# Rotary embedding over eight batch rows: from five homes and whole-row VectorE steps to six homes and quarter-row steps

## The chip, the core and the metric

The kernel runs on one core of a Trainium2 chip. The metric is the device time of one execution in microseconds (us); three timed runs of the kernel before gave 316.1, 316.19 and 316.19, median 316.19. The engines that matter here are VectorE (DVE), ScalarE (ACT), GpSimd (POOL), which also issues most of the transfers, SyncE (SP), which issues two, and the core's 16 DMA engines.

## The reference

`x` is float32 of shape (8, 2048, 16, 64): batch, position, head, head dimension. `cos` and `sin` are float32 of shape (2048, 32). Neighbouring elements of the head dimension form a pair that is rotated by the position's angle:

```python
x1, x2 = x_pairs[..., 0], x_pairs[..., 1]
out1 = x1 * cos - x2 * sin
out2 = x1 * sin + x2 * cos
out = np.stack([out1, out2], axis=-1)      # float32, shape of x
```

Input and output are 67.1 MB each, and 8.39 MB of each belong to one batch row.

## The kernel before, in words

Each of the 128 partitions holds K = 16 positions of a batch row, 1024 values each (16 heads of 64), so one row is 128 x 16384 values. In SBUF a row is kept as bf16 in a "home", a slice of the tile `xt`; there are NX = 5 homes, and `HOME` (L37) says which row lives where: rows 5, 6 and 7 take homes 0, 1 and 2 again. A load (L68 to L70, issued by POOL) casts float32 to bf16 in the transfer, a store (L72 to L74, POOL) casts back.

Row 0 is split at the start. Its first four positions come as float32 through SP's queue (L101) into a staging tile `head`, and ScalarE casts them (L108). Its other twelve (L102), `cos` (L103), `sin` (L104), rows 1 and 2 (L105) and rows 3 and 4 (L106) are queued by POOL one behind the other. VectorE makes two bf16 tables out of `cos` and `sin` (L110 to L112); `s_tab` has the sign folded in.

`rotate` (L76) then does a row in three VectorE instructions: `qt` = row times `s_tab` (L89), row times `c_tab` in place (L92), and row plus `qt` with the two of each pair swapped (L97). The tile `qt` is as large as a row. Row 0 is done as four positions and then twelve (L116, L117), all others as sixteen at once.

The order of the issues is written out by hand. The first store, of row 0 alone, is held back by two tiny ScalarE copies, called in the middle of row 2 (L119 to L122): the first reads the last element of row 2's `qt`, the second rewrites one element of home 0, which the store reads. A one-element POOL copy (`mark`, L126) reads the end of home 4, so that POOL waits for rows 3 and 4 to land. After it POOL issues the store of rows 1 and 2, the load of row 5 (L128, into row 0's home, so after row 0's store has landed) and of rows 6 and 7 (L129, after the store of rows 1 and 2 has landed), the store of rows 3 and 4 (L132) and of rows 5 and 6 (L136). POOL issues in this order and waits in it. Row 7 is cast by ScalarE to float32 in four pieces (L138) into `wide`, which lies over homes 3 and 4, and goes out through SP's queue in one store (L139).

Of the kernel before, what the change touches and what calls it, by code (L numbers as in the profile page):

```python
# [2 lines left out]

# [4 lines left out]


@with_exitstack  # L10
def kernel(
    ctx: ExitStack,
    tc: tile.TileContext,
    x: bass.AP,
    cos: bass.AP,
    sin: bass.AP,
    out: bass.AP,
):
    nc = tc.nc
    fp32 = mybir.dt.float32  # L20
    bf16 = mybir.dt.bfloat16
    mult = mybir.AluOpType.mult
    add = mybir.AluOpType.add

    B, S, H, D = x.shape
    P = 128
    K = S // P
    KP = 16
    D2 = D // 2
    HD = H * D  # L30
    NX = 5
    HEAD = 4
    PART = 4
    STAGE = 3


    HOME = [0, 1, 2, 3, 4, 0, 1, 2]  # L37

    x_t = x.rearrange("b (p k) h d -> b p k (h d)", p=P, k=K)
    out_t = out.rearrange("b (p k) h d -> b p k (h d)", p=P, k=K)  # L40
    x_r = x.rearrange("b (p k) h d -> p b (k h d)", p=P, k=K)
    out_r = out.rearrange("b (p k) h d -> p b (k h d)", p=P, k=K)
    cos_t = cos.rearrange("(p k) c -> p (k c)", p=P, k=K)
    sin_t = sin.rearrange("(p k) c -> p (k c)", p=P, k=K)

    consts = ctx.enter_context(tc.tile_pool(name="consts", bufs=1))
    stage = ctx.enter_context(tc.tile_pool(name="stage", bufs=1))

    xt = consts.tile([P, NX, K * HD], bf16)
    cos_sb = consts.tile([P, K * D2], fp32)  # L50
    sin_sb = consts.tile([P, K * D2], fp32)
    c_tab = consts.tile([P, K, D], bf16)
    s_tab = consts.tile([P, K, D], bf16)

    wide = (
        xt[:, STAGE : STAGE + 2]
        .rearrange("p a c -> p (a c)")
        .bitcast(fp32)
        .rearrange("p (k c) -> p k c", c=HD)
    )  # L60

    gate = consts.tile([1, 1], bf16)
    mark = consts.tile([1, 1], bf16)

    def home(b, k0=0, k1=K):
        return xt[:, HOME[b], k0 * HD : k1 * HD].rearrange("p (k c) -> p k c", c=HD)

    def load(b, n):  # L68
        h = HOME[b]
        nc.gpsimd.dma_start(out=xt[:, h : h + n], in_=x_r[:, b : b + n])  # L70

    def store(b, n):  # L72
        h = HOME[b]
        nc.gpsimd.dma_start(out=out_r[:, b : b + n], in_=xt[:, h : h + n])  # L74

    def rotate(b, k0=0, k1=K, between=None):  # L76
        nk = k1 - k0
        xp = home(b, k0, k1)
        qt = stage.tile([P, KP, HD], bf16, name="qt", tag="work")

        def rows(a):
            return a.rearrange("p k (h e) -> p k h e", h=H, e=D)

        def tab(a):
            return dataclasses.replace(
                a, offset=a.offset + k0 * D, ap=[a.ap[0], [D, nk], [0, H], [1, D]]
            )

        nc.vector.tensor_tensor(out=rows(qt[:, :nk]), in0=rows(xp), in1=tab(s_tab), op=mult)  # L89
        if between is not None:  # L90
            between(qt)
        nc.vector.tensor_tensor(out=rows(xp), in0=rows(xp), in1=tab(c_tab), op=mult)  # L92
        q_swap = dataclasses.replace(
            qt, offset=qt.offset + 1, ap=[qt.ap[0], [2, nk * HD // 2], [-1, 2]]
        )
        x3 = xp.rearrange("p k (a j) -> p (k a) j", j=2)
        nc.vector.tensor_tensor(out=x3, in0=x3, in1=q_swap, op=add)  # L97

    with tc.manual_schedule():
        head = stage.tile([P, HEAD, HD], fp32, name="st", tag="work")  # L100
        nc.sync.dma_start(out=head[:, :HEAD], in_=x_t[0, :, :HEAD])  # L101
        nc.gpsimd.dma_start(out=home(0, HEAD), in_=x_t[0, :, HEAD:])  # L102
        nc.gpsimd.dma_start(out=cos_sb, in_=cos_t)  # L103
        nc.gpsimd.dma_start(out=sin_sb, in_=sin_t)  # L104
        load(1, 2)  # L105
        load(3, 2)  # L106

        nc.scalar.copy(out=home(0, 0, HEAD), in_=head[:, :HEAD])  # L108
        s2 = s_tab.rearrange("p k (i j) -> p (k i) j", j=2)
        nc.vector.tensor_copy(out=s2[:, :, 0], in_=sin_sb)  # L110
        nc.vector.tensor_scalar_mul(s2[:, :, 1], sin_sb, -1.0)  # L111
        nc.vector.tensor_copy(  # L112
            out=c_tab.rearrange("p k (i j) -> p (k i) j", j=2),
            in_=cos_sb.to_broadcast([P, K * D2, 2]),
        )
        rotate(0, 0, HEAD)  # L116
        rotate(0, HEAD, K)  # L117

        def first_store(qt):  # L119
            nc.scalar.copy(out=gate, in_=qt[:1, KP - 1, HD - 1 :])  # L120
            nc.scalar.copy(out=xt[:1, HOME[0], :1], in_=xt[:1, HOME[0], :1])  # L121
            store(0, 1)  # L122

        rotate(1)
        rotate(2, between=first_store)
        nc.gpsimd.tensor_copy(out=mark, in_=xt[:1, 4, K * HD - 1 :])  # L126
        store(1, 2)
        load(5, 1)  # L128
        load(6, 2)  # L129
        rotate(3)  # L130
        rotate(4)
        store(3, 2)  # L132
        for b in range(5, B):
            rotate(b)
            if b == 6:
                store(5, 2)  # L136
        for k in range(0, K, PART):
            nc.scalar.copy(out=wide[:, k : k + PART], in_=home(B - 1, k, k + PART))  # L138
        nc.sync.dma_start(out=out_t[B - 1], in_=wide)  # L139


# [1 line left out]
_INS = ['x', 'cos', 'sin']  # L143
_OUTS = [((8, 2048, 16, 64), 'float32')]


# [23 lines left out]
```

## Time and profile before

| what | value |
|---|---|
| median of the timed runs | 316.19 us |
| the profiled execution's own time | 316.11 us |
| its span in the profile | 314.3 us |
| VectorE busy | 210.3 us (67%), 30 instructions |
| ScalarE busy | 19.3 us (6%), 8 instructions |
| POOL busy | 12.4 us (4%), 16 instructions |
| three VectorE instructions of a whole row | 8.69 us each |
| the same of four positions | 2.28 to 2.29 us each |

The profiled execution's own time is 1.8 us longer than its span, which starts with the first recorded instruction and ends with the last. The page gives, for each engine, busy time; then the span in 40 slices with the busy share of the DMA engines; the DMA queues; the chain of work that ended last; and groups of instructions with the idle time ahead of each and what ended it. Loads cast to bf16, and their bytes are counted at the smaller, bf16 side: a row is 4.19 MB as a load and 8.39 MB as a store, though as much of HBM is moved by each.

### The profile page before, as it was taken

The page shows a single profiled execution, that of the slowest core. Times are in us where ns is not written, and L with a number is a line of the kernel's source. Part 1 is how long each engine was busy: PE and PEld are TensorE (multiplying, and loading weights), DVE is VectorE, ACT ScalarE, POOL GpSimd, SP SyncE. Part 2 cuts the span into 40 slices and gives each one's busy share as a digit, 9 for nine tenths or more (in the row PEclk, how much of TensorE's full clock was granted, in tenths as well). Part 3 has the DMA queues.
Part 4 walks back from the last instruction along what each step waited for, and adds up shares of the span by engine and source line. Part 5 has one row for each costly group of instructions (what it writes and reads, how often), then busy time and mean ns, then how long its engine had stood idle before and what let it go on. Part 6 is the DMA issues. An engine that isn't in the chain of part 4 may idle for free.

```text
span 314.3 us, 114 instructions
## 1 busy us (share of the span) xinstructions
DVE 210.3 (67%) x30; ACT 19.3 (6%) x8; POOL 12.4 (4%) x16
## 2 busy tenths in 40 slices
DVE  0009995099999999999992299903999999200000
ACT  1030000000000000000000000000000000790000
POOL 4000000000002400000000000000000000000000
DMA  7999999999999999999999999999999999999996
GB/s 253 264 284 200 200 200 267 200 200 204 263 200 267 409 525 400 400 425 509 400 200 225 242 200 200 234 234 334 400 509 425 400 400 525 409 400 400 525 409 267
DMA packets 2512, 102.24 MB, mean 325 GB/s; under 512 B 208, under 2 KB 208, under 8 KB 336
## 3 DMA queue, kind: packets, MB, share of 16 engines
q0 software_dynamic: 2224, 91.75, 92.1%
q1 hardware_dynamic: 288, 10.49, 8.0%
HBM read 67.63 MB, written 67.11 MB: 429 GB/s over the span
## 4 chain that ended last, share of the span: by engine, by line
DVE 67%; another core or an unknown queue 11%; ACT 3%; ACTq 1%; issue 0%; DVEq 0%
DVE xt L92 22%; DVE xt L97 22%; DVE qt L89 22%; ACT xt L138 3%; ACTq L165 1%; DVE c_tab L112 0%; DVEq L89 0%; DVEq L92 0%
## 5 line engine op out<-in xcount | busy, mean ns | idle before, releaser
L89 DVE TENSOR_TENSOR qt<-xt,s_tab 128x16384 bf16<-128x16384 bf16 (+2 forms) x9 | 69.7, 7743 | 34.5 <-DMA xt<-in_x_dram 34.3
L92 DVE TENSOR_TENSOR xt<-xt,c_tab 128x16384 bf16<-128x16384 bf16 (+2 forms) x9 | 69.7, 7743 | 0.4
L97 DVE TENSOR_TENSOR xt<-xt,qt 128x16384 bf16<-128x16384 bf16 (+2 forms) x9 | 69.7, 7743 | 0.3
L138 ACT CAST xt<-xt 128x4096 f32<-128x4096 bf16 x4 | 14.1, 3601 | 171.7 <-DVE xt L97 171.7
L110 DVE CAST s_tab<-sin_sb 128x512 bf16<-128x512 f32 x1 | 0.5, 454 | 23.8 <-DMA sin_sb<-in_sin_dram 23.8
L74 POOL DMA_DIRECT2D out_dram<-xt x4 | 2.7, 670 | 184.9 <-ACT xt L121 93.4
L126 POOL COPY mark<-xt 1x1 bf16<-1x1 bf16 x1 | 5.0, 5019 | 2.6 <-DMA xt<-in_x_dram 2.6
L120 ACT COPY gate<-qt 1x1 bf16<-1x1 bf16 x1 | 0.2, 192 | 78.6 <-DVE qt L89 78.6
L70 POOL DMA_DIRECT2D xt<-in_x_dram x4 | 2.7, 696 | 43.1 <-DMA out_dram<-xt 43.1
L108 ACT CAST xt<-st 128x4096 bf16<-128x4096 f32 x1 | 3.6, 3605 | 13.1 <-DMA st<-in_x_dram 13.1
L108 ACT ACT_TABLE_LOAD x1 | 1.3, 1283 | 0.7 <-PEq L154 0.7
L102 POOL DMA_DIRECT2D xt<-in_x_dram x1 | 0.7, 680 | 0.8 <-PEq L165 0.8
L112 DVE CAST c_tab<-cos_sb 128x1024 bf16<-128x1024 f32 x1 | 0.7, 685 | 0.0
L103 POOL DMA_DIRECT2D cos_sb<-in_cos_dram x1 | 0.6, 569 | 0.0
L104 POOL DMA_DIRECT2D sin_sb<-in_sin_dram x1 | 0.6, 562 | 0.0
L111 DVE TENSOR_SCALAR s_tab<-sin_sb 128x512 bf16<-128x512 f32 x1 | 0.4, 444 | 0.0
L121 ACT COPY xt<-xt 1x1 bf16<-1x1 bf16 x1 | 0.2, 188 | 0.0
L154 POOL MEMSET const-float32-0.0<- 128x1 f32 x1 | 0.1, 99 | 0.2 <-issue 0.2
L154 POOL MEMSET const-bfloat16-1.0<- 128x1 bf16 x1 | 0.1, 102 | 0.0
L154 POOL MEMSET const-float32-1.0<- 128x1 f32 x1 | 0.1, 99 | 0.0
L154 POOL MEMSET const-uint8-127<- 128x1 uint8 x1 | 0.1, 99 | 0.0
## 6 DMA issues: line engine op xcount, KB each, us to landing
xt<-in_x_dram POOLq DMA_DIRECT2D x3, 8192.0 KB, 59.3
xt<-in_x_dram POOLq DMA_DIRECT2D x1, 4096.0 KB, 57.6
xt<-in_x_dram POOLq DMA_DIRECT2D x1, 3072.0 KB, 21.1
st<-in_x_dram SPq DMA_DIRECT2D x1, 2048.0 KB, 14.4
cos_sb<-in_cos_dram POOLq DMA_DIRECT2D x1, 256.0 KB, 21.2
sin_sb<-in_sin_dram POOLq DMA_DIRECT2D x1, 256.0 KB, 21.3
out_dram<-xt POOLq DMA_DIRECT2D x4, 49.9
out_dram<-xt SPq DMA_DIRECT2D x1, 30.0
```

What stands on the lines that cost most here:

```text
L70: nc.gpsimd.dma_start(out=xt[:, h : h + n], in_=x_r[:, b : b + n])
L74: nc.gpsimd.dma_start(out=out_r[:, b : b + n], in_=xt[:, h : h + n])
L89: nc.vector.tensor_tensor(out=rows(qt[:, :nk]), in0=rows(xp), in1=tab(s_tab), op=mult)
L92: nc.vector.tensor_tensor(out=rows(xp), in0=rows(xp), in1=tab(c_tab), op=mult)
L97: nc.vector.tensor_tensor(out=x3, in0=x3, in1=q_swap, op=add)
L102: nc.gpsimd.dma_start(out=home(0, HEAD), in_=x_t[0, :, HEAD:])
L103: nc.gpsimd.dma_start(out=cos_sb, in_=cos_t)
L108: nc.scalar.copy(out=home(0, 0, HEAD), in_=head[:, :HEAD])
L112: nc.vector.tensor_copy(out=c_tab.rearrange("p k (i j) -> p (k i) j", j=2), in_=cos_sb.to_broadcast([P, K * D2, 2]),)
L126: nc.gpsimd.tensor_copy(out=mark, in_=xt[:1, 4, K * HD - 1 :])
L138: nc.scalar.copy(out=wide[:, k : k + PART], in_=home(B - 1, k, k + PART))
L165: with _tile.TileContext(nc) as tc:
```

## The change

There are six homes in place of five. The staging tile, `cos` and `sin` have no tiles of their own any more; they lie in home 5 (`early`) until the load of row 5 overwrites them. `qt` holds four positions, and every row is done in four quarters, of three instructions each. The gate ahead of the first store now reads the end of row 2 after its last addition, and that store takes rows 0 and 1. The load of rows 3, 4 and 5 is one transfer. Stores are (0,1), (2,3), (4,5), then 6 through POOL and 7 through SP. Rows 6 and 7 are loaded one by one into homes 0 and 1. `mark` is gone. ScalarE casts row 7 quarter by quarter, each as soon as VectorE is through with it, into `wide`, which now lies over homes 2 and 3. In the core of the diff below, the lines that only rename are left out.

```diff
-    KP = 16
+    KP = 4
-    NX = 5
+    NX = 6
-    HOME = [0, 1, 2, 3, 4, 0, 1, 2]
+    HOME = [0, 1, 2, 3, 4, 5, 0, 1]
...
+    early = xt[:, NX - 1].bitcast(fp32)
+    head = early[:, : HEAD * HD].rearrange("p (k c) -> p k c", c=HD)
+    cos_sb = early[:, HEAD * HD : HEAD * HD + K * D2]
+    sin_sb = early[:, HEAD * HD + K * D2 : HEAD * HD + 2 * K * D2]
...
+    def rotate_row(b):
+        for k in range(0, K, KP):
+            rotate(b, k)
...
         load(1, 2)
-        load(3, 2)
...
-        rotate(0, 0, HEAD)
-        rotate(0, HEAD, K)
-
-        def first_store(qt):
-            nc.scalar.copy(out=gate, in_=qt[:1, KP - 1, HD - 1 :])
-            nc.scalar.copy(out=xt[:1, HOME[0], :1], in_=xt[:1, HOME[0], :1])
-            store(0, 1)
-
-        rotate(1)
-        rotate(2, between=first_store)
-        nc.gpsimd.tensor_copy(out=mark, in_=xt[:1, 4, K * HD - 1 :])
-        store(1, 2)
-        load(5, 1)
-        load(6, 2)
-        rotate(3)
-        rotate(4)
-        store(3, 2)
-        for b in range(5, B):
-            rotate(b)
-            if b == 6:
-                store(5, 2)
-        for k in range(0, K, PART):
-            nc.scalar.copy(out=wide[:, k : k + PART], in_=home(B - 1, k, k + PART))
-        nc.sync.dma_start(out=out_t[B - 1], in_=wide)
+        load(3, 3)
+        for b in range(3):
+            rotate_row(b)
+        nc.scalar.copy(out=gate, in_=home(2, K - 1, K)[:1, 0, HD - 1 :])
+        nc.scalar.copy(out=xt[:1, 0, :1], in_=xt[:1, 0, :1])
+        store(0, 2)
+        rotate_row(3)
+        store(2, 2)
+        load(6, 1)
+        load(7, 1)
+        rotate_row(4)
+        rotate_row(5)
+        store(4, 2)
+        rotate_row(6)
+        store(6, 1)
+        for k in range(0, K, KP):
+            rotate(7, k)
+            nc.scalar.copy(out=wide[:, k : k + KP], in_=home(7, k, k + KP))
+        nc.sync.dma_start(out=out_t[7], in_=wide)
```

More of the change, by code (lines that the diff above doesn't have):

```diff
@@ L27 @@
     K = S // P
-    KP = 16
+    KP = 4
     D2 = D // 2
     HD = H * D
-    NX = 5
+    NX = 6
     HEAD = 4
-    PART = 4
-    STAGE = 3
-    HOME = [0, 1, 2, 3, 4, 0, 1, 2]
+    HOME = [0, 1, 2, 3, 4, 5, 0, 1]
     x_t = x.rearrange("b (p k) h d -> b p k (h d)", p=P, k=K)
@@ L49 @@
     xt = consts.tile([P, NX, K * HD], bf16)
-    cos_sb = consts.tile([P, K * D2], fp32)
-    sin_sb = consts.tile([P, K * D2], fp32)
     c_tab = consts.tile([P, K, D], bf16)
     s_tab = consts.tile([P, K, D], bf16)
+    gate = consts.tile([1, 1], bf16)
+    early = xt[:, NX - 1].bitcast(fp32)
+    head = early[:, : HEAD * HD].rearrange("p (k c) -> p k c", c=HD)
+    cos_sb = early[:, HEAD * HD : HEAD * HD + K * D2]
+    sin_sb = early[:, HEAD * HD + K * D2 : HEAD * HD + 2 * K * D2]
     wide = (
-        xt[:, STAGE : STAGE + 2]
+        xt[:, 2:4]
         .rearrange("p a c -> p (a c)")
@@ L60 @@
     )
-    gate = consts.tile([1, 1], bf16)
-    mark = consts.tile([1, 1], bf16)
     def home(b, k0=0, k1=K):
@@ L74, in store, with rotate @@
         nc.gpsimd.dma_start(out=out_r[:, b : b + n], in_=xt[:, h : h + n])
[L76 to L79, printed above, removed]
+    def rotate(b, k0):
+        xp = home(b, k0, k0 + KP)
+        qt = stage.tile([P, KP, HD], bf16, name="qt", tag="qt")
         def rows(a):
@@ L85, in tab @@
             return dataclasses.replace(
-                a, offset=a.offset + k0 * D, ap=[a.ap[0], [D, nk], [0, H], [1, D]]
+                a, offset=a.offset + k0 * D, ap=[a.ap[0], [D, KP], [0, H], [1, D]]
             )
-        nc.vector.tensor_tensor(out=rows(qt[:, :nk]), in0=rows(xp), in1=tab(s_tab), op=mult)
-        if between is not None:
-            between(qt)
+        nc.vector.tensor_tensor(out=rows(qt), in0=rows(xp), in1=tab(s_tab), op=mult)
         nc.vector.tensor_tensor(out=rows(xp), in0=rows(xp), in1=tab(c_tab), op=mult)
         q_swap = dataclasses.replace(
-            qt, offset=qt.offset + 1, ap=[qt.ap[0], [2, nk * HD // 2], [-1, 2]]
+            qt, offset=qt.offset + 1, ap=[qt.ap[0], [2, KP * HD // 2], [-1, 2]]
         )
@@ L97, in rotate @@
         nc.vector.tensor_tensor(out=x3, in0=x3, in1=q_swap, op=add)
+    def rotate_row(b):
+        for k in range(0, K, KP):
+            rotate(b, k)
     with tc.manual_schedule():
-        head = stage.tile([P, HEAD, HD], fp32, name="st", tag="work")
-        nc.sync.dma_start(out=head[:, :HEAD], in_=x_t[0, :, :HEAD])
+        nc.sync.dma_start(out=head, in_=x_t[0, :, :HEAD])
         nc.gpsimd.dma_start(out=home(0, HEAD), in_=x_t[0, :, HEAD:])
@@ L105 @@
         load(1, 2)
-        load(3, 2)
-        nc.scalar.copy(out=home(0, 0, HEAD), in_=head[:, :HEAD])
+        nc.scalar.copy(out=home(0, 0, HEAD), in_=head)
         s2 = s_tab.rearrange("p k (i j) -> p (k i) j", j=2)
```

## The prediction, made before the changed kernel ran

> **What bounds the kernel now.** I read the page first: its slices and its DMA queues.
>
> ```profile
> DMA  7999999999999999999999999999999999999996
> q0 software_dynamic: 2224, 91.75, 92.1%
> q1 hardware_dynamic: 288, 10.49, 8.0%
> HBM read 67.63 MB, written 67.11 MB: 429 GB/s over the span
> DVE 67%; another core or an unknown queue 11%; ACT 3%; ACTq 1%; issue 0%; DVEq 0%
> ```
>
> The two queues' packets took 92.1% and 8.0% of the 16 DMA engines' span: together all of it. No slice but the first and the last is under 9. So the DMA engines never rest, and the span is the sum of the transfers. The last line is the chain of waits; it names VectorE, with 67%, but a chain follows who released whom, and VectorE waits three times for a load. I take the queue sums over the chain: a step of VectorE costs nothing so long as the DMA queue has the next transfer in hand when the one before ends. The whole question is whether it has, at each handover.
>
> Next the timeline, for the rate at which transfers end.
>
> ```profile
> 62.42 8.69 DVE L89 TENSOR_TENSOR qt<-xt,s_tab 128x16384 bf16<-128x16384 bf16 x1 [10.66 <-DMA xt<-in_x_dram]
> ...
> 97.32 0.19 ACT L120 COPY gate<-qt 1x1 bf16<-1x1 bf16 x1 [78.56 <-DVE qt L89]
> 97.33 8.69 DVE L92 TENSOR_TENSOR xt<-xt,c_tab 128x16384 bf16<-128x16384 bf16 x1
> 97.42 0.19 ACT L121 COPY xt<-xt 1x1 bf16<-1x1 bf16 x1
> 97.91 0.55 POOL L74 DMA_DIRECT2D out_dram<-xt  x1 [93.43 <-ACT xt L121]
> 101.04 5.02 POOL L126 COPY mark<-xt 1x1 bf16<-1x1 bf16 x1 [2.58 <-DMA xt<-in_x_dram]
> ...
> 120.67 0.57 POOL L70 DMA_DIRECT2D xt<-in_x_dram  x1 [4.92 <-DMA out_dram<-xt]
> ...
> 159.44 0.70 POOL L70 DMA_DIRECT2D xt<-in_x_dram  x1 [38.20 <-DMA out_dram<-xt]
> ```
>
> Rows 1 and 2 have landed at 62.42, rows 3 and 4 at 101.04: 38.62 for two, 19.31 a row. Row 0's store has landed at 120.67, that of rows 1 and 2 at 159.44: 38.77 for two, 19.4 a row. Sixteen row transfers of 19.3 to 19.4 are 309 to 310 us; with `cos`, `sin`, 1.7 us ahead of the first packet and about 1.2 behind the last that is the span.
>
> Last the windows of a quarter of a microsecond around the first handover from loads to stores. The two last columns are DMA share and GB/s; a packet is booked where it starts, so shares stand in bursts.
>
> ```profile
> 97.75:98.00 0.25, 0.25 (x1) 0.00 (x0) 0.09 (x1) 1.00 1.22 262
> 98.00:98.25 0.25, 0.25 (x1) 0.00 (x0) 0.25 (x1) 1.00 8.55 1835
> 98.25:98.50 0.25, 0.25 (x1) 0.00 (x0) 0.21 (x1) 1.00 0.00 0
> ...
> 100.25:100.50 0.25, 0.25 (x1) 0.00 (x0) 0.00 (x0) 1.00 3.69 1573
> 100.50:100.75 0.25, 0.25 (x1) 0.00 (x0) 0.00 (x0) 1.00 6.12 2622
> ```
>
> GB/s divided by the share tells loads from stores: 1835/8.55 is 215 (a load, counted in bf16), 2622/6.12 is 428 (a store). The last load packets start from 97.75 to 98.25, the first stores from 100.25 to 100.75, 2.45 later; a burst comes each 2.4 us while nothing is missing (19.3 us for eight of them), so there is no hole. The store that was issued at 97.91 was ready when the first engine came free, near 100.3.
>
> **The change, part by part.** All terms are set against the profiled execution's own 316.11 (span 314.3 and 1.8 around it), 0.08 under the median of 316.19.
>
> *Quarter steps on VectorE.* The four-position instructions of row 0 start at 25.05, 27.37, 29.69, and the next at 32.02: 2.32 each with the gap, against 8.73 for a whole row's (62.42 to 71.15). Four times 2.32 is 9.29, so a row is 27.87 in place of 26.18, 1.7 more. VectorE has 104 idle us in the span, and its work is covered by transfers, except where a store waits for it, below.
>
> *Loading three rows in one transfer, later.* The load of rows 3 to 5 overwrites `cos`, `sin` and the head, so POOL waits until the table casts end, at 25.1. Nothing is queued on POOL behind it but stores that come later still. The queue meanwhile works on rows 1 and 2, until 62: 37 us of cover, no cost. It ends one row later than the old load, at 101.04 + 19.31 = 120.35 by the landing, and its engines come free 0.3 to 0.8 before that (100.25 to 100.75 against 101.04): from 119.6 to 120.1, mean 119.8. Row 3 can't be used before the whole transfer lands, as its three rows share one wait: VectorE idles 118.2 to 120.4.
>
> *The first store, where the sum is decided.* Rows 1 and 2 now end at 62.42 + 24 x 2.32 = 118.1. The gate, which was released by row 2's first instruction, waits for its last. From there the old timeline holds: gate start 97.32 to issue 97.91 is 0.59, so POOL issues the store of rows 0 and 1 at 118.75. In the kernel before, the store was issued 2.4 before an engine came free; now 0.85 before the first and 1.05 before the mean. How long a POOL store takes from issue to its first packet when engines wait for it, the trace does not show. Bounds: it can't be over 2.45 for one row (97.91 to the first free engine, no hole); with a pair's issue of 0.70 in place of 0.55, 2.6. From below: SP's head load is issued at 0.74 and its first packets start in the slice 1.50 to 1.75, 1.0 after; its issue takes 0.37, so 0.63 remain behind it. POOL's 0.70 and 0.63 make 1.33; if packets start while the issue still runs, under 1.05, and then there is no hole. POOL's first load speaks for the longer side: issued at 1.25, its packets (215 GB/s a share) show only from 5.25 on, though behind some of the head's. I take the middle of 1.33 and 2.6, 1.97: the engines wait 1.97 - 1.05 = 0.9. A restart costs more than the wait: at the start of the span the first two bursts of packets lie about 1.1 apart, later ones 0.6, so the first packet is up to 0.5 longer; I take 0.2. Sum of this part: **+1.1 us**, from 0 to 2.0 (2.6 - 1.05 + 0.5). The queue is full from here to the end, so it goes into the time whole.
>
> [...]
>
> *The handovers behind it.* Row 3 is done at 120.5 + 12 x 2.32 = 148.4, and the store of rows 2 and 3 is issued at 148.7; the transfer ahead ends at 120 + 38.6 = 158.6: ten us of cover. If that cover is gone, lateness enters one for one. The load of row 6 waits for the first store to land, near 160, as the old load did; rows 2 and 3 go out until 197, so it is hidden, and so is row 7's, issued right behind. Rows 4 and 5 are done at 204.1; POOL's store of them is due at 236: 32 of cover. Row 6 lands at 217 and is done at 245, its store due at 275: 30. Row 7 is done at 273; ScalarE has only the last quarter's cast left (3.60), and SP issues at 277, while row 6's store runs until 294 even alone: 17. The two queues share the engines at the end, as before, where SP's store was issued at 283.46 and the share stood at 0.97 to 0.98 up to 310. The tail is the same.
>
> *What goes away:* the `mark` copy (5.02 on POOL) had 9 idle us behind it, worth nothing. No byte and no transfer is saved: 13 issues before, 13 after.
>
> Sum: 316.11 + 1.1 = **317.2 us**.
>
> **The rivals.**
>
> *No hole.* POOL's store is ready within about 1.05 us of its issue, or close enough that the hole stays under 0.7. For it: SP's 1.0; against: POOL's issue alone takes 0.70, and POOL's first load shows so late. It decides below a latency of 1.7. Time 316.1 to 316.8, not slower. Chance 0.34.
>
> *VectorE becomes late at the second store too.* If the quarter steps ran slower beside stores than the 2.32 that row 0 shows beside loads, row 3's twelve would use up the 10 us from 3.15 us a step on; at 3.3 the store would come 1.9 late, giving 319.1. Against: the whole-row steps took 8.69 beside loads (62.42) and beside stores (97.33) alike. Chance 0.04.
>
> *Faster.* If packets of a three-row load came closer than those of two-row ones, or the tail's two queues together moved more than 429 GB/s, a per cent of a row's 19.3 would be saved per row so moved; three rows would give 0.6, hence 315.5. Against: the DMA engines are at 100.1% by their own packets. Chance 0.03.
>
> **How the numbers follow.** The forecast, a hole at the first store and a time between 316.8 and 318.2, has 0.59. A measurement of this kernel tells about 0.2% from no change, 0.63 us: 315.6 to 316.8 counts as the same. Faster 0.03 (the last rival), same 0.34 (the no-hole rival), slower 0.63 (the forecast and late VectorE). The range runs from no hole, 316.1, to the bound of 2.0 us, 318.1, with 0.1 for the run's own spread: 316.1 to 318.2.
>
> **What would show it.** In the profile after: VectorE steps of 2.29 throughout, 221 us busy in all; POOL's first store issued near 118.75 with row 3 starting near 120.4; in fine windows around 120, a last burst of load packets near 117.4 and the first store burst 3.3 to 3.5 later rather than 2.4 (with no hole: near 119.8); every later burst 2.4 apart; DMA share sum a little under 100%; the span longer by just this hole. I am wrong if the store is issued before 118, if a hole shows elsewhere (148 to 160, or the tail), or if the packets themselves take another time than before.

## The result, and the profile after

The changed kernel takes 317.01 us (median of 9 runs, 316.94 to 317.23) against 316.19 us before: 0.82 us more, a ratio of 1.0026 with a 95% interval of 1.0017 to 1.0035. It is a little slower. The prediction said 317.2 within 316.1 to 318.2.

The profiled execution of the changed kernel took 317.23 us, the longest of the nine, with a span of 315.5; the spans of the others are 315.2 to 315.5. Its tables landed 0.25 us later than in the profile of before (VectorE's first cast starts at 24.02 against 23.77). This is the last of the 16 DMA engines and not all of them: by the packet starts in the trace, the engines' first full-size load packets (32,768 bytes) start at 23.20 on the mean, against 23.19 before, but the last of them at 23.63 against 23.32. The seven profiles of this kernel's variants below have the first cast at 23.76 to 23.91, those of the kernel before and its variants at 23.72 to 23.91. So the wider spread belongs to this one execution; it makes about 0.25 of the 1.2 us between the two spans.

The page's lines on the DMA engines, for the changed kernel:

```profile
DMA  8999999999999999999999999999999999999996
...
q0 software_dynamic: 2224, 91.75, 91.7%
q1 hardware_dynamic: 288, 10.49, 7.9%
q14 instruction: 1, 0.01, 0.0%
```

The same packets now fill 99.6% of the span in place of 100.1%. So some time is lost in which an engine has nothing to do. And there is a queue that the page of before does not have: q14, of the kind `instruction`, one packet; by the trace it has 8192 bytes and takes 0.34 us from 130.07 on. It is read here as code for one of the engines (an instruction fetch); the runs with added VectorE instructions, below, bear that out.

The timeline around the first store:

```profile
116.17 2.29 DVE L91 TENSOR_TENSOR xt<-xt,qt 128x4096 bf16<-128x4096 bf16 x1
118.49 0.19 ACT L115 COPY gate<-xt 1x1 bf16<-1x1 bf16 x1 [99.42 <-DVE xt L91]
118.59 0.19 ACT L116 COPY xt<-xt 1x1 bf16<-1x1 bf16 x1
119.08 0.73 POOL L71 DMA_DIRECT2D out_dram<-xt  x1 [92.39 <-ACT xt L116]
120.60 2.29 DVE L85 TENSOR_TENSOR qt<-xt,s_tab 128x4096 bf16<-128x4096 bf16 x1 [2.14 <-DMA xt<-in_x_dram]
```

POOL issues the store at 119.08, 0.33 later than forecast (118.75): VectorE waited for that last DMA engine and began row 1 at 62.67, not 62.42. The DMA engines' mean is not later. They come free at 119.78 (mean start of the last load packets, 117.35, and 2.43 that they took), as forecast (119.8). So the lead over the mean engine is 0.70 and not the forecast's 1.05. Windows of a quarter of a microsecond at the same place (engines' busy time, then the TensorE clock, DMA share and GB/s; a packet is booked where it starts):

```profile
117.00:117.25 0.25, 0.25 (x1) 0.00 (x0) 0.00 (x0) 1.00 3.04 655
117.25:117.50 0.25, 0.25 (x1) 0.00 (x0) 0.00 (x0) 1.00 4.87 1049
117.50:117.75 0.25, 0.25 (x1) 0.00 (x0) 0.00 (x0) 1.00 1.22 262
...
120.25:120.50 0.25, 0.00 (x0) 0.00 (x0) 0.00 (x0) 1.00 8.51 3670
120.50:120.75 0.25, 0.15 (x1) 0.00 (x0) 0.00 (x0) 1.00 1.22 524
```

The bursts give the number of packets: 655 GB/s for 0.25 us is 164 KB, five load packets of 32,768 bytes; 3670 is 14 store packets of 65,536. In the kernel before, the first stores started 2.45 us after the last loads. Here it is 3.08 on the mean of the 16 engines (packet starts in the trace). This is a hole of 0.63, at the place that was forecast. It also lines the engines up: the last loads started over 0.72 us, the first stores within 0.15. The engine that came free first lost about 0.9, the last one at most 0.3, and the last one sets the end.

The second loss was not forecast. The same view ten microseconds later:

```profile
130.00:130.25 0.25, 0.25 (x1) 0.00 (x0) 0.00 (x0) 1.00 9.27 3965
130.25:130.50 0.25, 0.25 (x1) 0.00 (x0) 0.00 (x0) 1.00 0.69 262
...
132.25:132.50 0.25, 0.25 (x1) 0.00 (x0) 0.00 (x0) 1.00 6.12 2621
132.50:132.75 0.25, 0.25 (x1) 0.00 (x0) 0.00 (x0) 1.00 3.06 1311
...
133.00:133.25 0.25, 0.25 (x1) 0.00 (x0) 0.00 (x0) 1.00 0.61 262
```

3965 GB/s for 0.25 us is 991 KB: 15 store packets (983 KB) and 8 KB more, the packet of q14. One of the 16 engines carries it, and this engine's store packet comes a window later, in the next burst two windows after the others. It never catches up, as every engine has the same work: by the trace the packets of 32,768 and 65,536 bytes come in 120 bursts of 16, one for each engine, up to the last. At the end of the span:

```profile
311.00:311.25 0.25, 0.00 (x0) 0.00 (x0) 0.00 (x0) 1.00 8.46 3670
311.25:311.50 0.25, 0.00 (x0) 0.00 (x0) 0.00 (x0) 1.00 0.60 262
...
311.75:312.00 0.25, 0.00 (x0) 0.00 (x0) 0.00 (x0) 1.00 0.60 262
```

Fifteen last packets start by 311.5, the sixteenth 0.6 after them, and the kernel waits for it. In the kernel before all sixteen lie within 0.34:

```profile
310.25:310.50 0.25, 0.00 (x0) 0.00 (x0) 0.00 (x0) 1.00 3.63 1573
310.50:310.75 0.25, 0.00 (x0) 0.00 (x0) 0.00 (x0) 1.00 6.04 2621
```

The other handovers went as forecast: the store of rows 2 and 3 was issued at 148.77 (148.7), row 6's at 246.26 (245), SP's at 277.53 (277), and none of them shows a hole.

### The profile page after: what moved, and what is told of

It reads as the page before. It is cut to its first block, busy times and chain, and to the rows that moved or that the text cites. A ratio compares the mean times of both kernels' runs of the same rounds, so it can differ in the third digit from the quotient of the medians.

```text
span 315.5 us, 185 instructions
## 1 busy us (share of the span) xinstructions
DVE 221.3 (70%) x99; ACT 19.6 (6%) x8; POOL 7.3 (2%) x15
## 4 chain that ended last, share of the span: by engine, by line
DVE 70%; another core or an unknown queue 8%; DMA 7%; ACT 1%; issue 1%; POOL 0%; DVEq 0%; PEldq 0%
DVE qt L85 23%; DVE xt L86 23%; DVE xt L91 23%; DMA xt<-in_sin_dram 7%; ACT xt L129 1%; POOL xt L99 0%; POOL xt L100 0%; DVE s_tab L106 0%; DVE s_tab L107 0%; DVEq L85 0%; DVE c_tab L108 0%; PEldq L156 0%
## 5 line engine op out<-in xcount | busy, mean ns | idle before, releaser
L85 DVE TENSOR_TENSOR qt<-xt,s_tab 128x4096 bf16<-128x4096 bf16 x32 | 73.3, 2292 | 26.4 <-DMA xt<-in_x_dram 25.4
L91 DVE TENSOR_TENSOR xt<-xt,qt 128x4096 bf16<-128x4096 bf16 x32 | 73.3, 2292 | 1.1
L86 DVE TENSOR_TENSOR xt<-xt,c_tab 128x4096 bf16<-128x4096 bf16 x32 | 73.3, 2292 | 1.1
L104 ACT CAST xt<-xt 128x4096 bf16<-128x4096 f32 x1 | 3.6, 3604 | 13.5 <-DMA xt<-in_x_dram 13.5
L108 DVE CAST c_tab<-xt 128x1024 bf16<-128x1024 f32 x1 | 0.7, 684 | 0.0
```

The lines of the kernel that those rows point to most:

```text
L85: nc.vector.tensor_tensor(out=rows(qt), in0=rows(xp), in1=tab(s_tab), op=mult)
L104: nc.scalar.copy(out=home(0, 0, HEAD), in_=head)
L108: nc.vector.tensor_copy(out=c_tab.rearrange("p k (i j) -> p (k i) j", j=2), in_=cos_sb.to_broadcast([P, K * D2, 2]),)
```

## The experiments

Theory A, formed on this profile, has two causes: the hole at the first store, and one instruction fetch that sets a single DMA engine back. Theory B: the hole is all of it. Theory C: neither, but the quarter steps or the start. The times of before that ran with these kernels have medians of 316.18 to 316.34.

**The changed kernel without a gate.**

```diff
-        nc.scalar.copy(out=gate, in_=home(2, K - 1, K)[:1, 0, HD - 1 :])
-        nc.scalar.copy(out=xt[:1, 0, :1], in_=xt[:1, 0, :1])
```

> The changed kernel without the two tiny ScalarE copies ahead of the first store, so that POOL issues it when row 1 is done, near 90.5, and not near 119. Theory A (two causes: the hole at the first store, 0.55 on the last DMA engine, and one 8192-byte instruction fetch near 130 that sets a single DMA engine back by 0.6): no hole near 120, the fetch still there with one engine ending 0.6 behind the other fifteen, time 316.4 to 316.7. Theory B (the hole is all of it, the fetch is absorbed): 316.1 to 316.3. Theory C (neither; quarter steps or another start cost it): 317.0.

It took 317.70 us, ratio 1.0044 (1.0032 to 1.0057): slower than with the gate, which no theory had. The store was issued at 90.69, and there is no hole; the windows show something else:

```profile
117.50:117.75 0.25, 0.25 (x1) 0.00 (x0) 0.00 (x0) 1.00 9.12 1442
117.75:118.00 0.25, 0.25 (x1) 0.00 (x0) 0.00 (x0) 1.00 4.17 655
...
120.75:121.00 0.25, 0.00 (x0) 0.00 (x0) 0.00 (x0) 1.00 4.30 1835
121.00:121.25 0.25, 0.00 (x0) 0.00 (x0) 0.00 (x0) 1.00 4.89 2097
```

1442 GB/s are 11 load packets, and their share of 9.12 is 0.83 for each, against 0.61 elsewhere. A share of one over 16 engines and 0.25 us is 4 us of packet time, so these last packets took 3.3 us each and not 2.43. This became theory D, which later kernels test: a store that is in the queue before the last load packets ahead of it start stretches them by 0.9. The fetch is there too, at 130.68.

**The kernel before in quarter steps.**

```diff
-        rotate(1)
-        rotate(2, between=first_store)
+        for k in range(0, K, 4):
+            rotate(1, k, k + 4)
+        for k in range(0, K, 4):
+            rotate(2, k, k + 4, between=first_store if k == 4 else None)
...
-            nc.scalar.copy(out=gate, in_=qt[:1, KP - 1, HD - 1 :])
+            nc.scalar.copy(out=gate, in_=qt[:1, 3, HD - 1 :])
```

Rows 3 to 7 are done in quarters in the same way.

> The kernel before with every row from 1 on in quarter steps, the first store gated on row 2's second quarter, so issued near 100.5 with an engine coming free near 100.3 or just after 99.8 if the gate is passed at its first multiplication; homes, loads and stores as before. Theory A: the fetch appears for VectorE's longer instruction stream and one DMA engine ends about 0.6 late, time 316.6 to 316.8, plus 0 to 1.5 if the first store's issue at 100 comes too late as well (a hole at 100.5 would show in the windows). Theory B: only such a hole counts, 316.2 without one. Theory C: 317.0 without a hole.

317.44 us, ratio 1.0037 (1.0025 to 1.0050). The store was issued at 100.17, and the engines came free from 100.70 on: first stores 2.93 after the last loads on the mean, a hole of 0.49. One fetch, at 173.75, sets one engine back by 0.5; it ends 0.45 behind the last of the others. In this profile the loads ahead of the hole had also lost 0.34 (the last load packets start at 98.42 on the mean, against 98.08 before; several between 81 and 94 us took 2.55 to 2.60 in place of 2.43). Why is open. It is a part of what this kernel takes more than the changed one. Both causes appear in the old order of rows and homes, so neither hangs on six homes or on the three-row load.

**The gate 9 us later.**

```diff
-        nc.scalar.copy(out=gate, in_=home(2, K - 1, K)[:1, 0, HD - 1 :])
+        rotate(3, 0)
+        nc.scalar.copy(out=gate, in_=home(3, KP - 1, KP)[:1, 0, HD - 1 :])
```

> The changed kernel with the gate ahead of the first store reading the end of row 3's first quarter in place of the end of row 2: VectorE reaches it near 127.6, so the store is issued near 128.1, 9.0 later. Theories A and B: the hole near 120 grows by 9.0 and nothing behind takes it up, so 326.0 (325.5 to 326.5). Theory C: the lateness is absorbed by later slack, 317 to 318.

325.60 us, ratio 1.0298 (1.0284 to 1.0312), 8.6 above the changed kernel. Theory C is out: what the first store is late by goes into the time. The store was issued at 128.08, 9.0 later; that 8.6 and not 9.0 came out is put down to the second cause, by these windows:

```profile
124.25:124.50 0.25, 0.25 (x1) 0.00 (x0) 0.00 (x0) 1.00 0.08 33
...
129.25:129.50 0.25, 0.25 (x1) 0.00 (x0) 0.00 (x0) 1.00 9.12 3932
129.50:129.75 0.25, 0.25 (x1) 0.00 (x0) 0.00 (x0) 1.00 0.61 262
```

33 GB/s are the 8 KB of the fetch alone: it falls into the hole, where it delays nobody, and the engines start the stores together and end within 0.15.

**Tiny VectorE instructions in the kernel before**: 69 one-element copies ahead of row 5, where VectorE waits 11.17 us for a load. With them it has 99 instructions, as in the changed kernel.

```diff
         store(3, 2)
+        for _ in range(69):
+            nc.vector.tensor_copy(out=mark2, in_=gate)
```

> [...] Theory A: one instruction fetch of 8192 bytes in the span, one DMA engine 0.6 behind, time 316.6 to 316.8. Theory B and C: 316.2, the copies being hidden in the idle time.

316.43 us against 316.18, ratio 1.0006 (0.9997 to 1.0015): by itself not clear of nothing, and under theory A's 316.6 to 316.8. The copies took 12.3 us in all, 0.18 each, and so outlast the wait: row 5 starts 1.2 later than before; no handover shows a hole. The profile has the fetch, at 175.45. The engine that it set back by 0.5 was one of the first of the 16, so it ends only 0.2 behind the one that was last before.

> The kernel before with 198 one-element VectorE copies, 60 ahead of row 1 and 69 ahead of rows 5 and 6 each, all within VectorE's waits for loads (0.14 each). Theory A: two or three instruction fetches of 8192 bytes, each of which sets one DMA engine back by 0.5; 316.5 if they fall on different engines, up to 317.5 if on one. Theory B (the fetch is absorbed): 316.2 to 316.3.

With 198 such instructions (60 ahead of row 1, 69 each ahead of rows 5 and 6; they read `c_tab` and not `gate`, and are busy for 0.14 each): 316.93 us, ratio 1.0025 (1.0016 to 1.0034). Two fetches, at 61.7 and 214.3, and both on one engine, which ends alone:

```profile
310.25:310.50 0.25, 0.00 (x0) 0.00 (x0) 0.00 (x0) 1.00 5.44 2359
310.50:310.75 0.25, 0.00 (x0) 0.00 (x0) 0.00 (x0) 1.00 2.42 1049
...
311.25:311.50 0.25, 0.00 (x0) 0.00 (x0) 0.00 (x0) 1.00 0.60 262
```

The first set it back by 0.51, the second by 0.54; it ends 0.78 behind the next. Homes, transfers and their order are those of before. VectorE's rows start later, row 1 by 0.7 (it waits for the engine that was set back), rows 5 and 6 by 1.7 and 1.4 (the copies outlast the wait), but no store comes too late for the DMA engines by it: the first, issued at 98.60 and so 1.6 ahead of the first free engine, follows its loads by 2.44, and no two bursts lie more than 2.46 apart on the mean, as before. So the fetches cost 0.75, less than theory A's 317.5 for two on one engine, and theory B is out.

**The lead of the first store.** Three kernels move the gate ahead, to row 2's last multiplication by `c_tab`, its last by `s_tab`, and the one by `s_tab` a quarter earlier:

```diff
         nc.vector.tensor_tensor(out=rows(xp), in0=rows(xp), in1=tab(c_tab), op=mult)
+        if between is not None:
+            between(xp[:1, KP - 1, HD - 1 :])
...
+        for k in range(0, K, KP):
+            rotate(2, k, first_store if k == K - KP else None)
```

> The changed kernel with the gate one VectorE instruction earlier, on row 2's last multiplication by the cosine table: the first store is issued near 116.75, 3.0 before an engine comes free (119.75), where the kernel before had 2.4. Theory A (hole and fetch): no hole, the last load packets still 2.43 long, the fetch near 130 remains with one engine about 0.5 late: 316.4 to 316.8. Theory D, from the run without a gate (a store that is in the queue before the last load packets start stretches them by 0.9): no stretch yet or a small one, as they start at 117.1, so about the same 316.6. Rival E (any early store costs 0.9 in this kernel, whatever its lead): 317.5.

> The same with the gate on row 2's last multiplication by the sine table: the store is issued near 114.4, 5.3 ahead. Theory A: 316.4 to 316.8. Theory D: the store's work is queued before the last load packets start, so these take 3.3 in place of 2.43, and 317.3 to 317.7. Rival E: 317.5.

> The same with the gate one quarter of row 2 earlier: the store is issued near 107.4, 12.3 ahead. Theory A: 316.4 to 316.8. Theories D and E: last load packets of 3.3, 317.3 to 317.7, as without a gate.

They took 316.81 (ratio 1.0018, 1.0009 to 1.0026), 317.74 (1.0041, 1.0029 to 1.0054) and 317.59 (1.0038, 1.0024 to 1.0051). The last two are too slow for the fetch alone (theory A's 316.4 to 316.8) and near theory D's 317.3 to 317.7. The first lies between, and so do its last load packets (2.45 to 3.2 us). A fourth kernel has no gate, and a tiny store early:

```diff
+        nc.sync.dma_start(out=out_t[7, :, K - 1, :D], in_=head[:, 0, :D])
         load(3, 3)
```

> The kernel without a gate, and in addition a tiny store (64 floats a partition, 32 KB, overwritten later by row 7's store) from SP near 15 us, so that the output has been written to once before the first large store. Theory F (the 0.9 in the last load packets is a first-store cost, of the first write to the output): gone, 316.4 to 316.8. Theory D (it comes from a store being queued long ahead, whatever went before): still there, 317.4 to 317.9.

317.54 us, ratio 1.0039 (1.0026 to 1.0052), the last loads as long as without it: theory F falls. The last kernel adds a delay to the first of these four, so that the lead (how long before the first DMA engine comes free the store is issued) comes near the old one:

```diff
             nc.scalar.copy(out=gate, in_=seen)
+            for _ in range(6):
+                nc.scalar.copy(out=gate, in_=gate)
```

> The kernel with the gate on row 2's last multiplication by the cosine table, and six more one-element ScalarE copies chained between the gate and the store, so that it is issued 0.6 to 1.5 later, with a lead of 1.7 to 2.5 over the first free engine as in the kernel before (2.4). Theories A and D together: neither a hole nor stretched packets (last load packets 2.43 to 2.46, first stores 2.45 behind), only the fetch left, 316.4 to 316.7, so lower than both the changed kernel (317.0) and the run with a lead of 3 (316.8). Rival E (any store that is early costs): 316.8 or more.

316.64 us, ratio 1.0016 (1.0007 to 1.0025). Its windows at the handover:

```profile
117.25:117.50 0.25, 0.25 (x1) 0.25 (x2) 0.00 (x0) 1.00 6.13 1311
...
119.50:119.75 0.25, 0.00 (x0) 0.00 (x0) 0.00 (x0) 1.00 4.29 1835
119.75:120.00 0.25, 0.00 (x0) 0.00 (x0) 0.00 (x0) 1.00 4.91 2097
```

Ten load packets of 0.61 each, so 2.45 us long, and the stores 2.46 behind on the mean: neither hole nor stretch. The fetch, at 129.44, is the one loss left that the trace shows: its engine ends 0.40 behind the next. In order of the lead (from the issue to the first engine that comes free if its last load takes 2.43; by the trace):

| kernel | lead, us | last loads to first stores, us | time, us |
|---|---|---|---|
| changed, no gate | 29.3 | 3.33 | 317.70 |
| changed, no gate, tiny early store | 29.1 | 3.46 | 317.54 |
| gate at the third `s_tab` step | 12.4 | 3.43 | 317.59 |
| gate at the last `s_tab` step | 5.4 | 3.46 | 317.74 |
| gate at the last `c_tab` step | 3.2 | 2.83 | 316.81 |
| before (no fetch; the store is of one row) | 2.4 | 2.45 | 316.19 |
| gate at the last `c_tab` step, with delay | 1.7 | 2.46 | 316.64 |
| before in quarter steps (the store is of one row) | 0.5 | 2.93 | 317.44 |
| changed | 0.4 | 3.08 | 317.01 |
| changed, gate later | -8.2 | 11.89 | 325.60 |

The first store pays on both sides: late, by a hole that grows with its lateness; early, by stretched loads of up to 1.0 on the mean. Rival E falls by the packets: with a lead of 1.7 none is stretched, with 3.2 a part of them. Its time of 316.8 or more is not excluded by the interval alone. Of theory D it is shown that a long lead and the stretch come together in four kernels; what makes the stretch is not.

## Why the prediction was right, and where it was wrong

*The bound* was read rightly. The DMA engines set the time, and 1.7 us more of VectorE a row delayed no transfer but at the one handover that was named.

*The place and the sign* of the hole were right, and so were the steps to the issue: VectorE's 2.32 a step and the old 0.59 from gate to issue. The issue came 0.33 late in this execution, as shown above, and the lead over the mean engine was 0.70 in place of 1.05.

*The size of the hole* was too large: 1.1 forecast, 0.63 measured on the mean of the engines, at most 0.3 on the last in the profile. Two terms were mis-sized, and a third step was wrong: the sum charged the wait of the mean engine to the time, though the last engine sets the end. The latency of POOL's store was taken as 1.97, the middle of 1.33 and 2.6; it is 1.30 (issue at 119.08, first packets at 120.38). With the forecast's lead of 1.05 the hole would have been near 0.25; the shorter lead of 0.70 makes the rest. The lower bound, made of POOL's own 0.73 and what SP shows behind its issue, was the answer: behind the issue's end, 0.57 here, 0.56 in the quarter-step kernel of before, 0.56 with the gate later. The late first packets of POOL at the start spoke for waiting behind the head's, as was noted, and should not have moved the choice. The 0.2 for a slow restart did not show: the first stores took 2.43, as at the other handovers.

*What was missing* is the instruction fetch. The prediction costed the quarter steps by their durations alone; that with 99 VectorE instructions in place of 30 an instruction packet of 8192 bytes comes through one of the 16 DMA engines within the span was no term of the sum. (ScalarE and POOL have 8 and 15 instructions, 8 and 16 before; and added VectorE instructions alone brought the fetch into the kernel before: one at 175.45 with 69 more, two at 61.7 and 214.3 with 198 more.) By the runs it is worth about as much as the hole: of the 0.82, 0.37 goes when the hole goes (317.01 to 316.64), and 0.45 is left. The intervals of these two ratios overlap, so the halves are rough. That the total came so near is luck: one term was too big by about what the missing one is worth.

*The no-hole rival* came true by its own condition: a latency below 1.7 (1.30) and a hole under 0.7 (0.63). There is a hole, but one so small that the prediction counted it with this rival and not with the forecast. The rival's time of 316.1 to 316.8 was missed because of the fetch, which neither had, and only with the fetch does the time fall into the forecast's 316.8 to 318.2. Of the signs, a first store burst 3.3 to 3.5 behind the last loads did not come (3.08), and the span is longer by more than the hole.

*The two other rivals* are not borne out: VectorE's steps took 2.29 beside loads and stores alike, and no transfer got faster (a load packet took 2.43, a store packet 2.42 to 2.45, as before).

## What to carry to other kernels

Where the DMA engines never rest, walk through the handovers of the queue and ask of each when the next transfer is issued against when the engines come free; here one that came 0.6 short cost part of a us in a kernel whose VectorE has over 90 us to spare. Count instructions too: here 99 VectorE instructions in place of 30 brought a fetch that left one DMA engine 0.6 behind, and as all engines have the same work, the slowest of them is the time. And "as early as possible" is not always the best time to issue: for the first store here leads of 1.7 us (two rows) and 2.4 us (one row) brought neither a hole nor a stretch, 0.4 and 3.2 did, and before more work is put in front of a gate, it pays to learn what the gate was there for.

## What the runs showed of the hardware that was not expected

The stretch of the last loads: with the first store queued 5.4, 12.4 or 29.3 us ahead, the last load packet on every engine took 3.0 to 3.7 us in place of 2.43; with 3.2 us it was 2.45 to 3.2, with 2.4 and 1.7 none. Later handovers from loads to stores do not show it: in the changed kernel the store of rows 4 and 5 stands 30 us in the queue behind the loads of rows 6 and 7, and follows them by 2.43. A tiny early store from SP did not take it away. What it is stays open; whether an early store on POOL's own queue would take it away was not tried.

The instruction fetch: one packet of 8192 bytes, 0.3 us long, sets its engine back by 0.5 to 0.7. It came after 41 to 44 recorded VectorE instructions in the changed kernel and its variants, after 57 in the quarter-step kernel of before, and after 66 and 200 in the kernel with 198 copies. The fetches came one packet at a time, and no run here shows from which count on one more is fetched.
